# The last block of two weight tiles per unit, multiplied in float32 as it was loaded

## The chip, the cores and the metric

The kernel runs on one core of a Trainium2 chip. The metric is device time in microseconds of one execution, lower being better; times are the median of several executions, and one further execution was taken with the hardware profiler.

## The reference, cut to what matters

A two-layer trunk on 256 tokens of width 1024 ends in a mixture of eight experts, of which each token takes two. What the change touches is this sum over the experts:

```python
logits = (t @ w_router).astype(F32)
top_val, top_idx = lax.top_k(logits, TOP_K)
top_w = jax.nn.softmax(top_val, axis=-1)
combine = jnp.sum(jax.nn.one_hot(top_idx, N_EXPERTS, dtype=F32) * top_w[..., None], axis=1)
out = jnp.zeros_like(t)
for e in range(N_EXPERTS):
    gt, up = jnp.split(t @ w_gate_up[e], 2, axis=-1)
    y = (jax.nn.silu(gt) * up) @ w_down[e]
    out = out + combine[:, e:e + 1].astype(t.dtype) * y
```

Everything is float32; an expert's inner width is 3584, and its three matrices together are 44 MB.

## The kernel before

**Stream of weights.** All weights lie in HBM as one stream of tiles of 128 x 2048 float32 (1 MB). The class `Weights` loads them through the SP queue into a ring of buffers named `raw`, and splits each into two tiles of type float32r: `hi` is a copy made by ScalarE (L189), `lo` is `raw` minus `hi`, made by VectorE (L192). There are three `hi` and three `lo` buffers (`HL = 3`), so a tile is split at most three tiles before TensorE uses it. As soon as VectorE has subtracted, the load for that `raw` buffer is issued (L194), before TensorE has touched the tile; SP waits for VectorE there.

**Experts and units.** An expert's tokens are gathered into a tile `xs`. Its width 3584 is cut into seven units of 512 columns (`Unit`, loop at L1475). A unit takes six tiles: 0 and 1 for the gate, 2 and 3 for the up product, 4 and 5 for the down product. Each tile holds four blocks of 128 x 512. The down tiles of a unit come behind the gate and up tiles of the next one, so on the engines a round is: the previous unit's activation is folded or transposed, then tiles 0 to 3 of this unit, then tiles 4 and 5 of the previous one.

**Few and many.** The number of tokens of an expert is read into registers of TensorE, ScalarE and VectorE, and `choose` branches on it (L1160). With more than 64 tokens ("many", L1282 to L1286), each block is multiplied three times: token-hi by weight-hi, token-lo by weight-hi, token-hi by weight-lo. With 64 or fewer ("few", L1294 and L1298), the 128 stationary columns hold the hi parts of 64 tokens and their lo parts side by side, so two products do: by weight-hi (512 columns at once, L1294) and by weight-lo (two halves of 256, L1298). In the trace the first, third, seventh and eighth expert are few, the other four are many.

**The activation of a few unit.** It goes through all three engines while tiles 0 to 3 are multiplied: TensorE adds the two halves of the stationary columns with 16 float32 products by a matrix `fold` (L1387); ScalarE applies SiLU, VectorE multiplies (`act`, L1391); ScalarE makes the hi part (L1394) and VectorE the lo part (`ahm`, L1395), which tile 4 needs. These small steps stand in the engines' queues between the splits of the weight tiles: the order of VectorE is the splits of tiles 0 to 3, `act`, the split of tile 4, `ahm`, the split of tile 5.

**What sets the order.** No scheduler does: the program is in the order in which Python emits it (`next` calls `split`, then `products` emits the multiplications).

Of the kernel before, what the change touches and what calls it, by code (L numbers as in the profile page):

```python
# [30 lines left out]
NJ = FFE // 512  # L31
# [105 lines left out]
class Weights:  # L137


    def __init__(self, nc, wts, pool, order, queue, side=None):  # L140
        self.nc, self.wts, self.order, self.queue, self.side = nc, wts, order, queue, side
        self.pool, self.ring, self.turn = pool, [(pool, "raw", RAW)] * RAW, 0
        self.loads = self.splits = self.used = 0
        self.raw, self.ready, self.late = [], [], []
        self.limit = self.fine = len(order)

# [29 lines left out]

    def pieces(self, parts):
# [13 lines left out]
        def rest(c):  # L191
            self.nc.vector.tensor_tensor(out=lo[:, c:c + w], in0=raw[:, c:c + w], in1=hi[:, c:c + w].bitcast(F32), op=ALU.subtract)  # L192
            if c + w == TW:
                self.issue()  # L194
# [3 lines left out]
    def split(self, parts=1):  # L198
        if self.splits >= len(self.order):
            return  # L200
        for first, rest in self.pieces(parts):
            first()
            if self.side is not None and parts == 1:
                self.late.append(rest)
                self.side.after(3, self.catch_up)
            else:
                rest()

    def catch_up(self):
# [3 lines left out]
    def next(self, held=0):  # L213

        while self.splits < min(self.used - held + HL, self.limit):
# [54 lines left out]
def trunk(ctx, tc, xT_in, memT_in, wts, gcols, grows, rows, lbl, router, cst_in, tab_in, u_in, msk_in, out):  # L270
# [903 lines left out]

    class Gather:
# [6 lines left out]
        def onehot(self):  # L1182
# [6 lines left out]
            if self.both:  # L1189
                self.n = nc.values_load(counts[0:1, 0, self.e:self.e + 1], engines=[EngineType.PE, EngineType.Activation, EngineType.DVE],  # L1190
                                        min_val=0, max_val=S, skip_runtime_bounds_check_because="a count of the 256 tokens")
            self.x = main.tile([P, 2, KB, P], F32R, tag="hh" if self.e % 2 == 0 else "hl", name="xs")
# [80 lines left out]
    def products(n, o, st, w, ks, first, last, lead=None, also=()):  # L1273


        wh, wl = (t.rearrange("p (k n) -> p k n", k=4) for t in w)
# [13 lines left out]
        def few():  # L1290
            if lead:
                lead[1]()
            for m, k in enumerate(ks):
                T.matmul(o, lhsT=st[0][:, k], rhs=wh[:, k], start=first and m == 0, stop=False)  # L1294
            parts = (slice(0, 512),) if lead else (slice(0, 256), slice(256, 512))
            for k in ks:
                for c in parts:
                    T.matmul(o[:, c], lhsT=st[0][:, k], rhs=wl[:, k, c], start=False, stop=last and k == ks[-1] and c == parts[-1])  # L1298
# [249 lines left out]

    experts(W, pos, cr, g0, start)
# [59 lines left out]
```

## Time and profile before

| | us |
|---|---|
| median of 3 runs (1436.91 to 1437.73) | 1437.0 |
| the profiled execution, its own time | 1438.49 |
| its span, first to last instruction | 1436.3 |

| engine | busy, us | share of the span |
|---|---|---|
| PE (matmul) | 1373.1 | 96% |
| PEld (weight load) | 1231.9 | 86% |
| DVE (VectorE) | 1183.7 | 82% |
| ACT (ScalarE) | 1010.9 | 70% |
| POOL | 13.4 | 1% |

The experts run from about 500 us to 1424 us of the span. PE's busy time in a profile counts a matrix product until its modelled end, so neighbours overlap: the pace of a row of products is read from the starts of two rows, or from the length of a group less the time of its last product. An average over the span hides that few and many experts have different limits.

### The profile page before, as it was taken

How to read it: one execution, taken by the hardware profiler on the slowest of the kernel's cores; microseconds unless marked ns; L12 is line 12 of the kernel's file. 1: busy time of each engine (PE TensorE's matmuls, PEld its weight loads, DVE VectorE, ACT ScalarE, POOL GpSimd, SP SyncE). 2: the span in 40 equal slices, each digit the busy share in tenths (PEclk: the TensorE clock that was granted, in tenths of full speed). 3: DMA queues.
4: the chain of work that ended last, by engine and by line, in shares of the span. 5: the costliest groups of instructions: out<-in, count | busy, mean ns of one | idle time of the engine just before them, and what ended most of it. 6: DMA issues, size and time to landing. Idle time of an engine off the chain costs nothing.

```text
span 1436.3 us, 23628 instructions
## 1 busy us (share of the span) xinstructions
PE 1373.1 (96%) x8719; PEld 1231.9 (86%) x8719; DVE 1183.7 (82%) x1194; ACT 1010.9 (70%) x1104; POOL 13.4 (1%) x21
## 2 busy tenths in 40 slices
PE   8999999999999999999999999999999999999986
PEld 7989999999999888888887888888888888888875
DVE  7875655556776699998899999889899988999997
ACT  5775434435844698877787987777777778899795
POOL 0000000000000000000000000000000000000000
PEclk9999999999999999999999999999999999999999
DMA  9333455545425599999999999999999999999991
GB/s 347 145 118 144 170 189 190 190 176 206 147 89 220 206 354 390 409 388 367 354 376 405 383 416 375 345 362 350 361 367 360 369 337 376 386 403 420 405 396 38
DMA packets 64179, 431.91 MB, mean 301 GB/s; under 512 B 7504, under 2 KB 8144, under 8 KB 13584
## 3 DMA queue, kind: packets, MB, share of 16 engines
q1 hardware_dynamic: 63792, 428.63, 77.5%
q8 instruction: 109, 1.79, 0.5%
q0 software_dynamic: 224, 1.05, 0.2%
q14 instruction: 54, 0.44, 0.1%
HBM read 428.60 MB, written 1.05 MB: 299 GB/s over the span
## 4 chain that ended last, share of the span: by engine, by line
PE 50%; DVE 5%; issue 5%; DMA 3%; ACT 1%; DVEq 0%; ACTq 0%; POOL 0%; SPq 0%
PE pa L1282 7%; PE pa L1284 7%; PE pa L1286 7%; PE pb L1294 4%; DVE lo L192 4%; PE pb L1298 3%; PE pb L1282 3%; PE pa L1294 3%; PE pb L1286 3%; PE pb L1284 3%; PE pa L1298 3%; DMA raw<-in_wts 3%; PE pc L1387 3%; PE pc L1376 1%; ACT hi L189 1%
## 5 line engine op out<-in xcount | busy, mean ns | idle before, releaser
L192 DVE TENSOR_TENSOR lo<-raw,hi 128x2048 fp32r<-128x2048 f32 (+2 forms) x423 | 919.6, 2192 | 120.6 <-ACT hi L189 115.5
L189 ACT ACTIVATE hi<-raw 128x2048 fp32r<-128x2048 f32 (+2 forms) x423 | 770.7, 1838 | 172.3 <-PE pa L1284 51.6
L1298 PEld LDWEIGHTS pa<-lo,xs 128*128 128x128 f32 x800 | 113.1, 189 | 14.6 <-DVE lo L192 3.9
L1294 PE MATMUL pa<-hi,xs 128*128 128x512 f32 x448 | 124.7, 399 | 0.8 <-issue 0.6
L1298 PE MATMUL pa<-lo,xs 128*128 128x256 f32 (+1 forms) x800 | 124.7, 295 | 0.6 <-DVE lo L192 0.5
L1282 PE MATMUL pa<-hi,xs 128*128 128x512 f32 x448 | 123.8, 398 | 0.0
L1284 PE MATMUL pa<-hi,xs 128*128 128x512 f32 x448 | 120.2, 390 | 0.0
L1286 PE MATMUL pa<-lo,xs 128*128 128x512 f32 x448 | 120.1, 390 | 0.0
L309 PE MATMUL pa<-dh,lo 128*128 128x256 f32 x352 | 99.2, 282 | 1.3 <-DVE lo L192 1.3
L1284 PEld LDWEIGHTS pa<-hi,xs 128*128 128x128 f32 x448 | 84.1, 188 | 18.2
L1286 PEld LDWEIGHTS pa<-lo,xs 128*128 128x128 f32 x448 | 84.1, 188 | 18.0
L307 PE MATMUL pa<-dh,hi 128*128 128x256 f32 x352 | 99.4, 282 | 0.0
L308 PE MATMUL pa<-dl,hi 128*128 128x256 f32 x352 | 99.1, 281 | 0.0
L1282 PEld LDWEIGHTS pa<-hi,xs 128*128 128x128 f32 x448 | 81.2, 188 | 15.2
L1294 PE MATMUL pb<-hi,ahm 128*128 128x512 f32 x224 | 66.0, 416 | 28.4 <-DVE ahm L1395 27.5
L307 PE MATMUL pa<-hh,hi 128*128 128x256 f32 x288 | 84.9, 295 | 7.5 <-ACT hi L189 6.9
L1294 PEld LDWEIGHTS pa<-hi,xs 128*128 128x128 f32 x448 | 78.2, 189 | 13.4 <-issue 1.5
L308 PE MATMUL pa<-hl,hi 128*128 128x256 f32 x288 | 82.6, 287 | 0.1
L309 PE MATMUL pa<-hh,lo 128*128 128x256 f32 x288 | 82.6, 287 | 0.0
L1294 PEld LDWEIGHTS pb<-hi,ahm 128*128 128x128 f32 x224 | 39.7, 196 | 38.9 <-issue 27.2
L1298 PEld LDWEIGHTS pb<-lo,ahm 128*128 128x128 f32 x448 | 63.5, 196 | 5.8 <-DVE lo L192 0.4
L309 PEld LDWEIGHTS pa<-dh,lo 128*128 128x128 f32 x352 | 66.3, 188 | 1.5 <-DVE lo L192 1.5
(295 smaller groups left out, 2402.2 us busy)
## 6 DMA issues: line engine op xcount, KB each, us to landing
raw<-in_wts SPq DMA_DIRECT2D x393, 1024.0 KB, 7.0
raw<-in_wts SPq DMA_DIRECT2D x14, 512.0 KB, 8.0
raw<-in_wts SPq DMA_DIRECT2D x16, 256.0 KB, 6.0
xT<-in_xT SPq DMA_DIRECT2D x4, 256.0 KB, 4.9
memT<-in_memT SPq DMA_DIRECT2D x1, 1024.0 KB, 13.4
out<-res SPq DMA_DIRECT2D x4, 256.0 KB, 2.7
uc<-in_utab POOLq DMA_DIRECT2D x1, 576.0 KB, 4.5
gain<-in_grows SPq DMA_DIRECT2D x4, 128.0 KB, 7.7
```

Of the source, the lines that this page charges most:

```text
L189: self.nc.scalar.activation(hi[:, c:c + w], raw[:, c:c + w], AF.Copy)
L192: self.nc.vector.tensor_tensor(out=lo[:, c:c + w], in0=raw[:, c:c + w], in1=hi[:, c:c + w].bitcast(F32), op=ALU.subtract)
L307: T.matmul(o, lhsT=sh, rhs=mh, start=first, stop=False)
L308: T.matmul(o, lhsT=sh, rhs=ml, start=False, stop=False)
L309: T.matmul(o, lhsT=sl, rhs=mh, start=False, stop=last)
L1282: T.matmul(o, lhsT=st[0][:, k], rhs=wh[:, k], start=first and m == 0, stop=False)
L1284: T.matmul(o, lhsT=st[1][:, k], rhs=wh[:, k], start=False, stop=False)
L1286: T.matmul(o, lhsT=st[0][:, k], rhs=wl[:, k], start=False, stop=last and m == len(ks) - 1)
L1294: T.matmul(o, lhsT=st[0][:, k], rhs=wh[:, k], start=first and m == 0, stop=False)
L1298: T.matmul(o[:, c], lhsT=st[0][:, k], rhs=wl[:, k, c], start=False, stop=last and k == ks[-1] and c == parts[-1])
L1376: T.transpose(out=self.o[:, f * P:(f + 1) * P], in_=self.su[:, f * P:(f + 1) * P], identity=ident)
L1387: T.matmul(self.o[:, m * n + f * HALF:m * n + (f + 1) * HALF], lhsT=src[:, f * P:(f + 1) * P], rhs=fold, start=True, stop=True)
```

## The change

In an expert with few tokens, tiles 1 and 4 of each unit are split only in their first three blocks (1536 of 2048 columns). The last block is multiplied in plain float32 from `raw`, by the same stationary columns read as float32; that product comes first in the tile. Two of the tile's three remaining weight-hi products are cut into halves of 256 columns, which makes the number of instructions twelve as before. Since the width of the split now hangs on the expert, the split of tiles 1 and 4 stands in a branch of its own on all three engines, for every expert. And since TensorE now reads `raw`, the next load into a buffer is emitted only after the tile's products have been emitted (`refill` in `next`), for all tiles of the experts.

```diff
@@ class Weights @@
+        self.refills, self.whole = 0, None
...
+    def refill(self):
+        self.refills += 1
+        self.issue()
...
         def rest(c):
             self.nc.vector.tensor_tensor(out=lo[:, c:c + w], in0=raw[:, c:c + w], in1=hi[:, c:c + w].bitcast(F32), op=ALU.subtract)
-            if c + w == TW:
-                self.issue()
+            if c + w == TW and self.whole is None:
+                self.refill()
...
     def split(self, parts=1):
         if self.splits >= len(self.order):
+            return
+        if self.whole is not None and parts == 1 and self.whole(self.order[self.splits], self.split_most):
             return
...
+    def split_most(self, choose):
+
+        raw = self.raw[0]
+        self.pieces(1)
+        hi, lo = self.ready.pop()
+        self.ready.append((hi, lo, raw))
+
+        def parts(c):
+            self.nc.scalar.activation(hi[:, :c], raw[:, :c], AF.Copy)
+            self.nc.vector.tensor_tensor(out=lo[:, :c], in0=raw[:, :c], in1=hi[:, :c].bitcast(F32), op=ALU.subtract)
+
+        choose(lambda: parts(TW), lambda: parts(TW - 512))
...
     def next(self, held=0):
 
+
+        while self.whole is not None and self.refills < self.used:
+            self.refill()
         while self.splits < min(self.used - held + HL, self.limit):
...
@@ products @@
-        wh, wl = (t.rearrange("p (k n) -> p k n", k=4) for t in w)
+
+        wh, wl, *raw = (t.rearrange("p (k n) -> p k n", k=4) for t in w)
+        assert not raw or ks == ALL4 and lead is None
...
-            for m, k in enumerate(ks):
-                T.matmul(o, lhsT=st[0][:, k], rhs=wh[:, k], start=first and m == 0, stop=False)
-            parts = (slice(0, 512),) if lead else (slice(0, 256), slice(256, 512))
-            for k in ks:
+            halves = slice(0, 256), slice(256, 512)
+            parts = (slice(0, 512),) if lead else halves
+            if raw:
+                T.matmul(o, lhsT=st[0][:, 3].bitcast(F32), rhs=raw[0][:, 3], start=first, stop=False)
+            split = ks[:3] if raw else ks
+            for m, k in enumerate(split):
+                for c in halves if raw and m else (slice(0, 512),):
+                    T.matmul(o[:, c], lhsT=st[0][:, k], rhs=wh[:, k, c], start=first and m == 0 and not raw, stop=False)
+            for k in split:
                 for c in parts:
-                    T.matmul(o[:, c], lhsT=st[0][:, k], rhs=wl[:, k, c], start=False, stop=last and k == ks[-1] and c == parts[-1])
+                    T.matmul(o[:, c], lhsT=st[0][:, k], rhs=wl[:, k, c], start=False, stop=last and k == split[-1] and c == parts[-1])
...
@@ before the experts @@
+    def whole(t, split):
+
+        n = count_of[(t - NT) // (6 * NJ)]
+        if (t - NT) % 6 not in (1, 4) or n is None:
+            return False
+        split(lambda many, few: choose(n, many, few))
+        return True
+
+    W.whole = whole
     experts(W, pos, cr, g0, start)
```

The order on VectorE shows it between the two steps of a unit's activation. Both arms of a branch stand there, many first and few second; `act` and `ahm` are the two steps of a few unit, `pads` belongs to many. Before:

```order
L1391 TENSOR_TENSOR act<-pc,act 128x256 [waits Activation_49]
L1164 UNCONDITIONAL_BRANCH
L192 TENSOR_TENSOR lo<-raw,hi 128x2048 [waits DMAHW6_49,PE_49,Activation_49]
L1164 COMPARE_AND_BRANCH
L1173 COPY pads<-few 128x1
L1164 UNCONDITIONAL_BRANCH
L1395 TENSOR_TENSOR ahm<-act,ahm 128x4x64 [waits Activation_49]
```

And now, at the same place:

```order
L1424 TENSOR_TENSOR act<-pc,act 128x256 [waits Activation_49]
L1187 UNCONDITIONAL_BRANCH
L1187 COMPARE_AND_BRANCH
L225 TENSOR_TENSOR lo<-raw,hi 128x2048 [waits DMAHW6_49,PE_49,Activation_49]
L1187 UNCONDITIONAL_BRANCH
L225 TENSOR_TENSOR lo<-raw,hi 128x1536 [waits DMAHW6_49,PE_49,Activation_49]
L1187 UNCONDITIONAL_BRANCH
L1187 COMPARE_AND_BRANCH
L1196 COPY pads<-few 128x1
L1187 UNCONDITIONAL_BRANCH
L1428 TENSOR_TENSOR ahm<-act,ahm 128x4x64 [waits Activation_49]
```

The split of tile 4 keeps its place and its waits; it now stands in two widths inside a branch.

On TensorE, tile 1 of a unit (`pa` is the sum in PSUM, `xs` the tokens), both arms, before:

```order
L1164 COMPARE_AND_BRANCH
L1282 MATMUL pa<-hi,xs 128x512 x4
L1284 MATMUL pa<-hi,xs 128x512 x4
L1286 MATMUL pa<-lo,xs 128x512 x4
L1164 UNCONDITIONAL_BRANCH
L1294 MATMUL pa<-hi,xs 128x512 x4
L1298 MATMUL pa<-lo,xs 128x256 x8
```

And now, with the empty branch of the next whole tile's split behind it:

```order
L1187 COMPARE_AND_BRANCH
L1310 MATMUL pa<-hi,xs 128x512 x4
L1312 MATMUL pa<-hi,xs 128x512 x4
L1314 MATMUL pa<-lo,xs 128x512 x4
L1187 UNCONDITIONAL_BRANCH
L1324 MATMUL pa<-raw,xs 128x512
L1328 MATMUL pa<-hi,xs 128x512
L1328 MATMUL pa<-hi,xs 128x256 x4
L1331 MATMUL pa<-lo,xs 128x256 x6
L1187 UNCONDITIONAL_BRANCH
L1187 COMPARE_AND_BRANCH
L1187 UNCONDITIONAL_BRANCH x2
```

The arm for many is unchanged; in the arm for few one product from `raw` leads, and three products fewer use the last block's split.

On SP, the queue of the loads, six loads of the experts' stretch before:

```order
L157 DMA raw<-in_wts 128x2048 [waits DMAHW3_49,DVE_49]
L1164 UNCONDITIONAL_BRANCH
L157 DMA raw<-in_wts 128x2048 [waits DMAHW4_49,DVE_49]
L1164 UNCONDITIONAL_BRANCH
L157 DMA raw<-in_wts 128x2048 [waits DMAHW5_49,DVE_49]
L1164 UNCONDITIONAL_BRANCH
L157 DMA raw<-in_wts 128x2048 [waits DMAHW6_49,DVE_49]
```

And now:

```order
L158 DMA raw<-in_wts 128x2048 [waits DMAHW3_49,DVE_49]
L1187 UNCONDITIONAL_BRANCH x2
L158 DMA raw<-in_wts 128x2048 [waits DMAHW4_49,PE_49]
L1187 UNCONDITIONAL_BRANCH
L158 DMA raw<-in_wts 128x2048 [waits DMAHW5_49,DVE_49]
L1187 UNCONDITIONAL_BRANCH
L158 DMA raw<-in_wts 128x2048 [waits DMAHW6_49,DVE_49]
L1187 UNCONDITIONAL_BRANCH x2
```

The loads behind a whole tile wait for TensorE instead of VectorE, and the loads queued after them on SP stand behind that wait.

## Rows read from the trace of the kernel before

**Rows 1.** Windows: few, few, many, last two few; us, PE, PEld, DVE, ACT, POOL, PEclk, DMA, GB/s
```profile
500.60:602.40 101.80, 94.19 (x596) 83.80 (x596) 95.25 (x67) 90.11 (x80) 0.00 (x0) 0.98 0.95 373
724.30:833.70 109.40, 101.72 (x630) 89.99 (x629) 103.22 (x76) 93.41 (x82) 0.00 (x0) 0.98 0.99 389
833.70:1203.20 369.50, 369.50 (x1725) 307.16 (x1724) 329.57 (x230) 278.27 (x247) 0.00 (x0) 1.00 0.95 363
1203.20:1401.80 198.60, 183.21 (x1147) 162.81 (x1146) 191.17 (x138) 171.72 (x147) 0.00 (x0) 0.99 1.00 399
```

**Rows 2.** Windows of one unit each, of few experts, the same columns
```profile
724.30:740.50 16.20, 15.01 (x90) 13.18 (x89) 14.80 (x11) 13.54 (x12) 0.00 (x0) 1.00 0.98 364
740.50:755.70 15.20, 15.05 (x93) 13.20 (x92) 15.20 (x14) 13.21 (x11) 0.00 (x0) 1.00 0.97 365
755.70:770.90 15.20, 13.45 (x86) 11.82 (x85) 14.79 (x10) 12.81 (x10) 0.00 (x0) 1.00 0.99 398
770.90:787.80 16.90, 15.11 (x85) 13.00 (x84) 16.44 (x14) 13.13 (x11) 0.00 (x0) 0.90 1.01 421
787.80:805.20 17.40, 16.88 (x115) 15.29 (x114) 14.33 (x12) 15.22 (x20) 0.00 (x0) 1.00 0.97 381
...
1325.70:1344.20 18.50, 16.68 (x94) 14.54 (x93) 18.50 (x16) 14.08 (x11) 0.00 (x0) 0.91 1.02 411
...
1358.20:1372.70 14.50, 13.18 (x85) 11.85 (x84) 14.08 (x10) 12.84 (x11) 0.00 (x0) 1.00 1.02 422
```

**Rows 3.** Waits in that last unit: waiting engine and line, releaser: us, times, longest
```profile
PE pb L1294 <- DVE ahm L1395: 1.3, 1, 1.3
```

**Rows 4.** Waits over all experts, 500.6 to 1401.8 us
```profile
PE pb L1294 <- DVE ahm L1395: 26.0, 20, 1.8
...
DVE lo L192 <- DMA raw<-in_wts: 3.5, 8, 0.9
```

**Rows 5.** Timeline, plain few unit: start us, us, engine, line, instructions, [idle before]
```profile
1358.85 1.92 ACT L189 ACTIVATE hi<-raw 128x2048 fp32r<-128x2048 f32 x1 [0.55 <-PE pa L1294]
...
1359.56 1.07 PE L1294 MATMUL pa<-hi,xs 128*128 128x512 f32 x4
...
1360.46 1.11 PE L1298 MATMUL pa<-lo,xs 128*128 128x256 f32 x8
...
1361.42 1.09 PE L1294 MATMUL pa<-hi,xs 128*128 128x512 f32 x4
...
1363.55 0.42 DVE L1391 TENSOR_TENSOR act<-pc,act 128x256 f32<-128x256 f32 x1
1363.88 2.28 DVE L192 TENSOR_TENSOR lo<-raw,hi 128x2048 fp32r<-128x2048 f32 x1
...
1366.08 0.42 DVE L1395 TENSOR_TENSOR ahm<-act,ahm 128x256 fp32r<-128x256 f32 x1
...
1366.65 1.16 PE L1294 MATMUL pb<-hi,ahm 128*128 128x512 f32 x4 [1.32 <-DVE ahm L1395]
...
1371.32 1.06 PE L1387 MATMUL pc<-fold,svm 128*128 128x64 f32 x8
```

**Rows 6.** Timeline, then line view, of a float32 product of 256 columns
```profile
26.41 0.59 PE L366 MATMUL pc<-dg,cst 128*128 128x256 f32 x2
...
L366 PE MATMUL pc<-dg,cst x8: 377/378/483, 26.4 to 354.4; 128*128 128x256 f32 x8
```

**Rows 7.** Splits by tile, last two experts: ns min/median/max; the shortest have 1024 columns
```profile
L189 ACT ACTIVATE hi<-raw x82: 1049/1912/1977, 1201.1 to 1401.1; 128x2048 fp32r<-128x2048 f32 x76, 128x1024 fp32r<-128x1024 f32 x6
L192 DVE TENSOR_TENSOR lo<-raw,hi x79: 1217/2284/2294, 1203.1 to 1400.5; 128x2048 fp32r<-128x2048 f32 x76, 128x1024 fp32r<-128x1024 f32 x3
```

**Rows 8.** Loads in the plain unit
```profile
DMA packets 830, 6.09 MB, mean 419 GB/s; under 512 B 88, under 2 KB 88, under 8 KB 88
```

**Rows 9.** Branches in the stretch of three many experts, ns min/median/max
```profile
L1164 PEldq COMPARE_BRANCH  x276: 65/172/344, 848.8 to 1202.5; - x138
```

**Rows 10.** Window inside the unit at 770.9, columns of rows 1
```profile
779.00:784.00 5.00, 3.79 (x14) 3.40 (x15) 4.59 (x5) 5.00 (x4) 0.00 (x0) 0.67 1.02 423
```

More of the change, by code (lines that the diff above doesn't have):

```diff
@@ L1173, in pad_dve @@
         V.tensor_copy(pads[:, 8:9], one)
+    count_of = {}
     class Gather:
@@ L1191, in onehot @@
                                         min_val=0, max_val=S, skip_runtime_bounds_check_because="a count of the 256 tokens")
+                count_of[self.e] = self.n
             self.x = main.tile([P, 2, KB, P], F32R, tag="hh" if self.e % 2 == 0 else "hl", name="xs")
```

## The prediction

> **What bounds the kernel now.** I read the windows by stage first. Experts with many tokens are bound by TensorE: in the three that follow each other PE is busy for all of the 369.5 us [rows 1]. The change leaves the products of those units alone, so their pace should stay. The four few experts take 101.8 + 109.4 + 198.6 = 409.8 us, of which PE is busy 379.1: it stands idle for 30.7 us. That idle time is all that the change can win, beside a slow clock in it.
>
> Next, one unit at a time [rows 2]. A plain few unit (the row at 1358.2; eight others look like it, at 14.5 to 15.5 us) takes 14.5: VectorE is busy 14.1, PE 13.2, ScalarE 12.8. PE stands still once, for 1.3 us, at the first down product, which waits for `ahm` from VectorE [rows 3]; over all experts this wait has 26.0 us in 20 places [rows 4]. The timeline shows why [rows 5]: `act` comes at 1363.55 behind the split of tile 3, then the split of tile 4 runs from 1363.88 for 2.28 us, then `ahm` at 1366.08, and PE, done with tile 3, starts tile 4 at 1366.65 after 1.32 us idle. So a few unit is bound by VectorE's queue, and PE is next, only 1.3 us behind. Weights bind nothing: VectorE waited for a load 3.5 us in all [rows 4].
>
> Units with more to do differ. At 740.5 (scatter of the last expert) and 787.8 (gather of the next) PE is busy 15.05 of 15.2 and 16.88 of 17.4. At 770.9 (a one-hot to build on VectorE) and 1325.7 the granted clock averages 0.90 and 0.91 [rows 2]; inside the first of them it is 0.67 over 5 us, a mixture of the levels 2.4 and 1.2 GHz, just after PE has stood still [rows 10]. A third unit, in the first expert, is like it.
>
> **The change part by part.** *Splits.* 1536 columns lie midway between the 1024 and 2048 that have rows [rows 7]: VectorE (1217 + 2284)/2 = 1.75 us, 0.53 less; ScalarE (1049 + 1912)/2 = 1.48, 0.43 less. Per unit, with two such tiles, VectorE falls to about 13.0 us and ScalarE to 12.0.
>
> *The float32 product.* No row has one of 512 columns. The nearest is L366, 256 columns: the one instruction shows as two records, 0.59 us together, and one alone takes 0.378 [rows 6]; so the second begins 0.21 us after the first. For 512 columns I double that: two records of 0.43, 0.85 us. It replaces one weight-hi product, (1360.46 - 1359.56)/4 = 0.225, and two weight-lo halves of (1361.42 - 1360.46)/8 = 0.12 each [rows 5]; cutting two other products into halves adds 4 x 0.12 - 2 x 0.225 = 0.03. Net +0.85 - 0.225 - 0.24 + 0.03 = **+0.42 us of PE per whole tile**. Bounds: the weight load of such a product is hidden beside L366, but where float32 products are short it sets the pace, 1.06/8 = 0.13 us each (L1387 [rows 5]). Two loads wholly unhidden would make it +0.68. From below: L366's records follow each other 0.21/0.12 as slowly as float32r products of as many columns; from 0.225 that ratio gives 2 x 0.39 = 0.79, or +0.36. I take +0.42, since a product of 512 columns covers a load better than one of 256 does. There are 28 few units, 56 such tiles, less four that are split before the switch is set or belong to the last eight tiles, which are split in pieces: 52, so 22 us of PE work against 30.7 us of idle time.
>
> *The wait for ahm.* PE reaches tile 4 0.42 us later (tile 1 is longer). `ahm` comes earlier: by 0.53 from tile 4's shorter split, and by up to 0.53 more from tile 1's, if the split of tile 3 can start earlier. It can: its ScalarE half runs 1358.85 to 1360.77 [rows 5], VectorE's half ended only with `act`'s start at 1363.55, so began about 1361.3; 0.5 us are there. So 1.32 - 0.42 - 0.53 - 0.5 is below zero; the wait goes, PE is late next. A plain unit then lasts 13.2 + 0.84 = 14.05; I write 14.2, for what the chain may leave: 0.34 less, in nine units.
>
> *The clock.* In the units at 770.9 and 1325.7 and the first expert's, the longer idle stretch shrinks by the same 1.45 us. I expect the clock to stay at 2.4 GHz there: waits of 1.3 us in plain units don't lower it now (1.00 [rows 2]). Without the slow stretch PE's work at 770.9 would be a plain unit's 13.2, plus 0.84, plus about a microsecond behind the one-hot: 15.1 against 16.9, twice. At 1325.7 it has the products of the unit at 740.5: 15.05 + 0.84, with 0.3 to spare 16.2 against 18.5.
>
> *Where PE binds already* it only loses. Three gather units: 16.9 + 0.84 + 0.1 = 17.8 against 17.2 on average, +0.6 each. The two scatter units at 740.5 and its like: +0.7, but the units behind them, which waited 1.8 us (13.45 busy of 15.2), go to 14.3: -0.2 a pair. Units at a border of few and many have one whole tile and no wait to win: four times +0.4.
>
> *Branches and loads.* Each engine takes two more branches a unit. In many experts PE has seven a unit already, 276 records of 65 to 344 ns in some 21 units, 1.9 to a branch, on its sequencer [rows 9], with no idle time at all [rows 1], so they run ahead of the array; the same holds on VectorE beside splits of 2 us. Only behind the short `act` might 0 to 0.2 us show: 26 x 0.05, +1. The next load waits for TensorE's first product of a whole tile rather than VectorE's split, some 1 to 4 us later of a ring that VectorE practically never waits for: nothing, unless the lead is used up (below).
>
> A page's rule speaks against the branches. The Trainium skill, Runtime: NRT & Kernel Launch, section Instruction fetch mechanics, says that a taken branch out of the fetched window stalls the engine for a fetch; by it every added branch would cost. This trace disagrees as far as it reaches, with 369.5 us busy of 369.5; the sum stands on the rows.
>
> *The sum:* plain units 9 x -0.34 = -3.1; slow-clock units -1.8 -1.8 -2.3 = -5.9; pairs 2 x -0.2 = -0.4; gathers +1.8; borders +1.6; branches +1.0. Together -5.0, so the profiled span of 1436.3 becomes 1431.3. Its execution took 1438.49, 1.5 above the median of 1437.0; the difference carried to the median gives **1432.0 us**.
>
> **The rivals.** *The chain stays late.* If `act` hangs on something that doesn't move (ScalarE starts tile 3's copy only when PE frees a buffer, 0.55 us idle [rows 5]), VectorE's chain wins 0.53 alone: the wait becomes 1.32 - 0.42 - 0.53 = 0.37, a plain unit 14.4 (9 x -0.1), and the clock still falls (3 x -0.5); pairs turn to +0.3 each. -0.9 - 1.5 + 0.6 + 1.8 + 1.6 = +1.6: 1438.6. For it: VectorE and ScalarE wait for each other and for PE's buffers. Against it: the gap between 1360.77 and 1361.3.
>
> *The float32 product costs more* (slower). If both its weight loads show, 52 x 0.26 = 13.5 more: 1445.5. It decides from 0.1 us a tile (5.0/52). Against: the two records of L366 follow at 0.21 us, which their columns fill.
>
> *Branches show on PE* (slower): 112 branches of 1.9 records at 0.17 (the median [rows 9]) are 36: 1468 at most, were the skill's rule to hold.
>
> *Loads bind.* A unit's 6.29 MB at 419 GB/s [rows 8] take 15.0 us, longer than my 14.2. What carries the few experts is the lead that the many leave. If it runs out in the last two, their gain (3.6) goes: 1435.6. By the skill's HBM Reference (Specifications), a core's share is 358 GB/s, 17.6 us a unit, while a core alone gets about 425; this trace agrees with the second.
>
> *It doesn't do what it says* (no expert takes the branch): 1437. The few rows in four experts speak against it.
>
> *More comes back:* no idle time left in few units but at their borders, 1426.5.
>
> **How the numbers follow.** Chances: forecast 0.45 (its own range 1428.5 to 1434), more back 0.10, late chain 0.20, loads 0.05, no effect 0.03, costlier product 0.12, branches 0.05. A measurement can tell about 0.2%, 2.9 us, from no change: faster (below 1434.1) 0.55, within 0.28, slower 0.17. The range of 1426 to 1443 leaves out the branches, most of the costlier product, and little below.
>
> **What would show it.** Right: the line of `raw` products shows two records each at 0.43 us; splits of 1536 columns take 1.75 and 1.48 us; the wait of the first down product for `ahm` falls from 26 us to under 8; the granted clock is 1.00 in the one-hot units; gather units get longer; PE stays busy all through the many experts. Wrong: a wait for `ahm` that stays, waits for loads in the last expert, idle PE in many experts, or records of `raw` products further apart than 0.5 us.

## The result, and the profile after

| | before | after |
|---|---|---|
| median, us | 1437.29 | 1426.33 |
| lowest to highest of 4 runs | 1436.91 to 1437.73 | 1425.91 to 1426.99 |
| span of the profiled execution | 1436.3 | 1424.1 |

The ratio of after to before is 0.9924, with a 95% interval of 0.9907 to 0.9941: faster by 11 us. The forecast was 1432.0, in a range of 1426 to 1443; the time is at the low end of the range, below the 1428.5 to 1434 of the forecast itself, and all but equal to the rival "more comes back" (1426.5), which had a chance of 0.10.

By stage, cut where the work of [rows 1] stands (columns as there):

```profile
500.60:598.87 98.27, 96.71 (x609) 83.19 (x609) 88.87 (x67) 85.16 (x81) 0.00 (x0) 1.00 0.94 374
721.20:827.00 105.80, 104.05 (x643) 89.38 (x642) 97.00 (x76) 88.57 (x82) 0.00 (x0) 1.00 0.99 402
827.00:1196.93 369.93, 369.93 (x1726) 307.22 (x1725) 328.55 (x230) 277.60 (x247) 0.00 (x0) 1.00 0.93 363
1196.93:1389.60 192.67, 190.33 (x1172) 162.60 (x1171) 178.57 (x137) 161.79 (x147) 0.00 (x0) 1.00 1.01 409
```

The three many experts still keep PE busy throughout; the 0.4 us more there belongs to the border with the few expert ahead of them. The few experts together take 396.7 us instead of 409.8, and PE, busy for 391.1 of them, stands idle for 5.7 us where it stood for 30.7.

One unit at a time, from the start of one unit's fold to that of the next. In order: a gather, the two of a pair (scatter, then the unit behind it), a one-hot unit, the first unit of the last expert that was slow, and a plain one:

```profile
551.03:568.71 17.68, 17.42 (x118) 15.29 (x117) 15.24 (x13) 14.71 (x19) 0.00 (x0) 1.00 1.01 416
735.14:750.80 15.66, 15.66 (x95) 13.43 (x94) 14.88 (x14) 13.02 (x12) 0.00 (x0) 1.00 0.96 370
750.80:764.64 13.84, 13.84 (x88) 11.87 (x87) 12.55 (x10) 11.57 (x10) 0.00 (x0) 1.00 0.97 388
764.64:779.53 14.89, 14.07 (x89) 11.92 (x88) 13.89 (x13) 12.02 (x11) 0.00 (x0) 1.00 1.01 412
...
1314.93:1331.32 16.39, 15.91 (x97) 13.36 (x96) 16.39 (x16) 13.46 (x13) 0.00 (x0) 1.00 1.01 417
1345.39:1359.39 14.00, 14.00 (x88) 11.91 (x87) 13.05 (x10) 12.02 (x11) 0.00 (x0) 1.00 1.02 421
```

The plain unit takes 14.00 us and PE is busy for all of it; before it took 14.5, with 1.3 of idle PE [rows 2]. The clock is 1.00 in the two units that showed 0.90 and 0.91.

Waits over all experts, the lines that answer [rows 4]:

```profile
PE pb L1324 <- issue: 3.2, 5, 0.8
...
DVE lo L197 <- DMA raw<-in_wts: 2.7, 3, 0.9
...
DVE lo L225 <- DMA raw<-in_wts: 1.1, 1, 1.1
```

No line names a wait of PE for `ahm` any more; it was 26.0 us. In part only the name is lost: the first product of tile 4 is now the one from `raw` (L1324), for which the profile names no releaser ("issue"), and in half of the few units it starts 0.10 us after `ahm` is done, as in the timeline below. What PE idles ahead of it is 3.2 us in five places. VectorE's waits for loads are 3.8 us, as before (3.5). Splits and float32 products by tile (L224 and L225 hold both arms; L1324 is the product from `raw`):

```profile
L224 ACT ACTIVATE hi<-raw x108: 1470/1905/1926, 507.0 to 1379.1; 128x2048 fp32r<-128x2048 f32 x56, 128x1536 fp32r<-128x1536 f32 x52
L225 DVE TENSOR_TENSOR lo<-raw,hi x108: 1745/2278/2294, 509.2 to 1381.0; 128x2048 fp32r<-128x2048 f32 x56, 128x1536 fp32r<-128x1536 f32 x52
...
L1324 PE MATMUL pa<-raw,xs x52: 590/591/595, 511.9 to 1377.4; 128*128 128x512 f32 x52
```

There are 52 short splits, 26 of tile 1 and 26 of tile 4, of 1.47 and 1.75 us at their shortest. The line of L1324 holds tile 1's 26 products, with two records each. Last, the timeline of the plain unit, the counterpart of [rows 5]:

```profile
1349.03 1.02 PE L1324 MATMUL pa<-raw,xs 128*128 128x512 f32 x2
...
1349.48 1.27 PE L1328 MATMUL pa<-hi,xs 128*128 128x512 f32 x5
...
1350.59 0.88 PE L1331 MATMUL pa<-lo,xs 128*128 128x256 f32 x6
...
1351.31 1.09 PE L1328 MATMUL pa<-hi,xs 128*128 128x512 f32 x4
...
1352.63 0.42 DVE L1424 TENSOR_TENSOR act<-pc,act 128x256 f32<-128x256 f32 x1
1352.97 1.75 DVE L225 TENSOR_TENSOR lo<-raw,hi 128x1536 fp32r<-128x1536 f32 x1
...
1353.14 0.42 ACT L1427 ACTIVATE ahm<-act 128x256 fp32r<-128x256 f32 x1 [0.58 <-DVE act L1424]
...
1353.46 0.67 ACT L1389 ACTIVATE sgm<-pa,cs 128x512 f32<-128x512 f32 x1
...
1354.04 1.90 ACT L194 ACTIVATE hi<-raw 128x2048 fp32r<-128x2048 f32 x1
...
1354.63 0.41 DVE L1428 TENSOR_TENSOR ahm<-act,ahm 128x256 fp32r<-128x256 f32 x1
...
1355.15 1.10 PE L1324 MATMUL pb<-raw,ahm 128*128 128x512 f32 x2
...
1355.97 2.29 DVE L197 TENSOR_TENSOR lo<-raw,hi 128x2048 fp32r<-128x2048 f32 x1 [0.92 <-ACT hi L194]
...
1366.63 0.42 DVE L1424 TENSOR_TENSOR act<-pc,act 128x256 f32<-128x256 f32 x1
```

Two records of 0.59 us that take 1.02 together start 0.43 apart. The whole tile 1 lasts from 1349.03 to 1351.31, 2.28 us; before, a tile's products took from 1359.56 to 1361.42 [rows 5], 1.86: the product costs PE 0.42. And VectorE now waits 0.92 us ahead of tile 5's split, for ScalarE; before, in the unit of [rows 5], it was 0.39:

```profile
1366.89 2.29 DVE L192 TENSOR_TENSOR lo<-raw,hi 128x2048 fp32r<-128x2048 f32 x1 [0.39 <-ACT hi L189]
```

### The profile page after: what moved, and what is told of

The parts are those of the page before. It is cut to its first block, busy times and chain, and to the rows that moved or that the text cites. A ratio compares the mean times of both kernels' runs of the same rounds, so it can differ in the third digit from the quotient of the medians.

```text
span 1424.1 us, 24320 instructions
## 1 busy us (share of the span) xinstructions
PE 1386.0 (97%) x8771; PEld 1230.6 (86%) x8771; DVE 1156.5 (81%) x1194; ACT 989.8 (70%) x1104; POOL 13.4 (1%) x21
## 4 chain that ended last, share of the span: by engine, by line
PE 62%; issue 1%; DVE 1%; ACT 1%; POOL 0%; DVEq 0%; ACTq 0%
PE pa L1310 7%; PE pa L1312 7%; PE pa L1314 7%; PE pa L1328 7%; PE pa L1331 6%; PE pb L1310 4%; PE pb L1314 4%; PE pb L1312 4%; PE pc L1420 3%; PE pb L1331 3%; PE pb L1328 3%; PE pb L1324 2%; PE pa L1324 2%; PE pc L1409 1%; PE pc L1225 1%
## 5 line engine op out<-in xcount | busy, mean ns | idle before, releaser
L197 DVE TENSOR_TENSOR lo<-raw,hi 128x2048 fp32r<-128x2048 f32 (+2 forms) x315 | 677.1, 2159 | 125.2 <-ACT hi L194 120.7
L194 ACT ACTIVATE hi<-raw 128x2048 fp32r<-128x2048 f32 (+2 forms) x315 | 567.5, 1810 | 141.6 <-PE pa L1312 42.9
L225 DVE TENSOR_TENSOR lo<-raw,hi 128x2048 fp32r<-128x2048 f32 (+1 forms) x108 | 219.0, 2027 | 10.0 <-ACT hi L224 8.7
L224 ACT ACTIVATE hi<-raw 128x2048 fp32r<-128x2048 f32 (+1 forms) x108 | 184.8, 1711 | 43.9 <-PE pb L1312 19.1
L1328 PE MATMUL pa<-hi,xs 128*128 128x512 f32 (+1 forms) x474 | 129.8, 397 | 0.5 <-issue 0.3
L1310 PE MATMUL pa<-hi,xs 128*128 128x512 f32 x448 | 123.8, 398 | 0.0
L1312 PE MATMUL pa<-hi,xs 128*128 128x512 f32 x448 | 120.2, 390 | 0.0
L1331 PE MATMUL pa<-lo,xs 128*128 128x256 f32 (+1 forms) x748 | 117.7, 295 | 0.5 <-DVE lo L197 0.5
L1331 PEld LDWEIGHTS pa<-lo,xs 128*128 128x128 f32 x748 | 105.8, 189 | 10.2 <-DVE lo L197 0.9
L1328 PEld LDWEIGHTS pa<-hi,xs 128*128 128x128 f32 x474 | 79.9, 189 | 22.9 <-issue 13.6
L1314 PEld LDWEIGHTS pa<-lo,xs 128*128 128x128 f32 x448 | 84.1, 188 | 18.0
L1328 PE MATMUL pb<-hi,ahm 128*128 128x512 f32 (+1 forms) x250 | 66.5, 391 | 2.4 <-ACT hi L194 2.4
```

What stands on the lines that cost most here:

```text
L194: self.nc.scalar.activation(hi[:, c:c + w], raw[:, c:c + w], AF.Copy)
L224: self.nc.scalar.activation(hi[:, :c], raw[:, :c], AF.Copy)
L225: self.nc.vector.tensor_tensor(out=lo[:, :c], in0=raw[:, :c], in1=hi[:, :c].bitcast(F32), op=ALU.subtract)
L1312: T.matmul(o, lhsT=st[1][:, k], rhs=wh[:, k], start=False, stop=False)
L1314: T.matmul(o, lhsT=st[0][:, k], rhs=wl[:, k], start=False, stop=last and m == len(ks) - 1)
L1328: T.matmul(o[:, c], lhsT=st[0][:, k], rhs=wh[:, k, c], start=first and m == 0 and not raw, stop=False)
```

## Two theories

**TensorE.** What the prediction held: the two short splits together took the wait for `ahm` away, and TensorE's own work (0.42 us longer for each whole tile) is what a few unit takes now.

**Row A.** A few unit is paced by a closed row of steps that VectorE and ScalarE hand to each other: `act` (VectorE), hi part of `ahm`, `sgm`, hi part of tile 5 (ScalarE), then lo parts of tiles 5, 0, 1, 2, 3 (VectorE), and `act` again. In the timeline above: `act` at 1352.63, tile 5's lo part at 1355.97 (3.34 later), the next `act` at 1366.63 (10.66 later), 14.00 in all; before, 3.34 and 11.20. Tile 1's lo part is in it, tile 4's stands beside it (VectorE would only wait longer ahead of tile 5). So half of the change, tile 1's 0.53 us, would bring all of a plain unit's gain: 14.53 to 14.00, with TensorE near its bound by chance. In the experiments that ran first this theory is called "round".

The totals of the experiments also hold what lies ahead of the first few unit's fold. In the profiled executions this fold starts at 507.96 us before, at 508.15 after, and between 508.64 and 513.53 in the others; from 500 to 510 us the granted clock is 1.00 in some and 0.84 to 0.88 in others. The lengths of units don't hold that.

The lengths that the experiments gave, in us, from the first product of one unit's fold to that of the next (from the timelines; the plain unit is the last expert's fifth, the one-hot units those of the first and third expert, the border unit is the third expert's first):

| | plain | one-hot, one-hot | gather | border |
|---|---|---|---|---|
| before | 14.53 | 16.90, 16.96 | 17.16 | 15.24 |
| after | 13.98 | 14.91, 14.89 | 17.68 | 15.26 |
| branches alone | 14.54 | 16.99, 15.43 | 17.21 | 15.25 |
| float32 product, full splits | 14.59 | 15.21, 15.45 | 17.67 | 15.28 |
| short splits, no float32 product | 13.99 | 14.90, 14.90 | 17.17 | 15.25 |
| tile 4 alone | 14.55 | 15.44, 15.44 | 17.57 | 15.25 |
| tile 1 alone | 14.19 | 14.72, 14.89 | 17.18 | 15.28 |
| short split on VectorE alone | 14.06 | 14.67, 14.68 | 17.68 | 15.28 |
| before, `sgm` one step later | 14.63 | 15.53, 15.53 | 17.21 | 15.26 |
| tile 1 alone, `sgm` one step later | 14.18 | 14.81, 15.01 | 17.15 | 15.28 |
| tile 3 alone | 14.01 | 14.91, 14.89 | 16.84 | 14.38 |
| before, copies behind tiles 0 and 1 | 14.67 | 15.29, 15.27 | 17.84 | 15.38 |
| tile 3 alone, copies behind tiles 0 and 1 | 14.43 | 14.75, 14.75 | 17.62 | 14.38 |
| tile 3 alone, copies placed anew | 13.75 | 14.30, 14.41 | 16.83 | 14.39 |

## The experiments

### Parts of the change

**Branches alone.** Both arms split in full, and no product takes `raw`; the branches and the later loads stay.

```diff
-        self.ready.append((hi, lo, raw))
+        self.ready.append((hi, lo))
...
-        choose(lambda: parts(TW), lambda: parts(TW - 512))
+        choose(lambda: parts(TW), lambda: parts(TW))
```

> The splits of tiles 1 and 4 stand in their branches and the loads are issued late, as in the changed kernel, but both arms split all 2048 columns and no float32 product is made: the products are those of before. All theories that put the gain on the shorter splits: plain few units stay at 14.5 us, the wait for ahm at about 26 us in all, 1437 us within 2. If later loads or the branches themselves moved something: away from 1437 by more than 3 us, and many units off their 16.8.

Measured: 1437.34 us, ratio to before 0.9997 (0.9988 to 1.0007). The plain unit is 14.54: branches and later loads cost nothing that can be seen. The clock was the surprise. Windows of three units, the first expert's one-hot, the third's, and the slow one of the last:

```profile
538.26:555.25 16.99, 15.19 (x86) 13.06 (x85) 16.52 (x14) 13.84 (x12) 0.00 (x0) 0.90 0.99 396
769.86:785.29 15.43, 13.64 (x87) 11.72 (x85) 14.95 (x13) 12.88 (x11) 0.00 (x0) 1.00 1.01 419
1323.32:1340.26 16.94, 15.12 (x95) 13.20 (x94) 16.94 (x16) 14.35 (x13) 0.00 (x0) 1.00 1.02 418
```

The first runs at 0.90 as in the kernel before; in the other two the clock did not fall, though PE idles as long (1.8 us) and no work was taken away. 1.5 us of what each such unit can win is thus the clock's, and it does not take this change to win it. (In the last expert the unit behind it gave 1.1 us back, 14.00 to 15.12, so the total hardly moved.)

**The float32 product without the short split.** Both arms split in full; the block is multiplied from `raw` all the same.

```diff
-        choose(lambda: parts(TW), lambda: parts(TW - 512))
+        choose(lambda: parts(TW), lambda: parts(TW))
```

> The float32 product is made as in the changed kernel, but all 2048 columns are split as before. Theory shorter splits: nothing is gained, plain few units stay at 14.5 us (the added 0.4 us per tile goes into the idle time of TensorE), units bound by TensorE pay: 1440 to 1443 us. Rival, that the float32 product itself brings the gain, since it comes first in the tile, needs no split and fills TensorE's wait: near 1427.

Measured: 1440.27 us, ratio 1.0017 (1.0007 to 1.0027), as expected: the product by itself brings nothing. Where TensorE is not the bound it hides (plain 14.59, +0.05); where it is, it costs 0.3 to 0.6 (gather 17.67). The three units that had the slow clock ran at 1.00 here, at 15.21, 15.45 and 16.92 us, which hides a part of the price in the total.

**The short split without the float32 product.** The last block of a whole tile is left out of the sum; the third block is multiplied again in its place, so that the number and kind of products are those of before.

```diff
-            if raw:
-                T.matmul(o, lhsT=st[0][:, 3].bitcast(F32), rhs=raw[0][:, 3], start=first, stop=False)
-            split = ks[:3] if raw else ks
...
+            blocks = (0, 1, 2, 2) if raw else ks
```

> Splits of 1536 columns as in the changed kernel, no float32 product: the third block is multiplied a second time in the place of the last, so TensorE's work is that of before (the last block of tiles 1 and 4 is left out of the sum in few experts). Theory round: VectorE and ScalarE go round from act over the copy of tile 5 to the splits of tiles 5, 0, 1, 2, 3 and back to act, 14.53 us, of which only tile 1's split got shorter, by 0.53: plain units 14.0, and no cost on TensorE, about 1423 us. Theory TensorE: with the wait for ahm gone a plain unit lasts TensorE's 13.1 to 13.4 us: 1414 to 1417.

Measured: 1423.59 us, ratio 0.9903 (0.9887 to 0.9920). The plain unit, as a window, and its wait of TensorE:

```profile
1357.16:1371.15 13.99, 13.49 (x86) 11.77 (x85) 13.04 (x10) 12.01 (x11) 0.00 (x0) 1.00 1.01 413
```

```profile
PE pb L1324 <- DVE ahm L1424: 0.4, 1, 0.4
```

Without the 0.84 us of the float32 products PE idles 0.5 us, and the unit is no shorter: 14.0. So 14.0 is not TensorE's figure, though after the change TensorE's work fills it as well.

**Tile 4 alone, tile 1 alone.**

```diff
-        if (t - NT) % 6 not in (1, 4) or n is None:
+        if (t - NT) % 6 != 4 or n is None:
```

and the same with `!= 1`.

> Only tile 4 of a unit gets the short split and the float32 product; tile 1 is as before. Theory round: tile 4's split is not in the round, VectorE only idles longer before tile 5's split (0.39 + 0.53 us); plain units stay at 14.5, units bound by TensorE pay 0.4 each: 1436 to 1439 us. Theory TensorE: the wait for ahm falls from 1.32 to 0.79, tile 4 costs 0.40: plain units 14.25 to 14.4, 1433 to 1435 us.

Tile 4 alone: 1434.35 us, ratio 0.9974 (0.9965 to 0.9984), plain unit 14.55. PE idles less ahead of tile 4 all the same, 0.91 us instead of 1.32, and 15.4 instead of 26.0 over all experts; the product that waits starts 0.10 us after `ahm` is done, so the wait has only lost its name. Tile 5's split waits 0.9 us instead of 0.39:

```profile
1366.64:1381.19 14.55, 13.64 (x88) 11.87 (x86) 13.60 (x10) 12.46 (x11) 0.00 (x0) 1.00 0.99 392
```

```profile
1376.43 0.42 DVE L1428 TENSOR_TENSOR ahm<-act,ahm 128x256 fp32r<-128x256 f32 x1
...
1376.95 1.10 PE L1324 MATMUL pb<-raw,ahm 128*128 128x512 f32 x2 [0.91 <-issue]
```

```profile
DVE lo L197 <- ACT hi L194: 0.9, 1, 0.9
```

The total lies where the theory "TensorE" had it, the plain unit does not (14.25 to 14.4). The 3 us lie in the one-hot units (15.44, no shorter than the 15.43 of branches alone at a clock of 1.00) and in the second unit of each pair (14.40 instead of 15.12), which the first form of row A had not counted.

> As the changed kernel, but only tile 1 of a unit is whole; tile 4 is split in full, in no branch. Theory round (VectorE and ScalarE hand each other the steps of a few unit in one closed row, in which only tile 1's shorter split lies): a plain few unit still takes 14.0 us, as with both tiles, since tile 4's split stands outside the round; units where TensorE binds pay for one tile instead of two (gathers +0.2 instead of +0.4). Total 1422 to 1425, faster than the changed kernel. Theory halves (each of the two short splits brings its share): the plain unit goes half the way, 14.25, and the total lies near 1431. Theory TensorE (what was won is the wait for ahm, and the float32 product is the next bound): with half its price the plain unit falls below 14.0, to 13.6.

Tile 1 alone: 1428.78 us, ratio 0.9943 (0.9926 to 0.9959), and a plain unit of 14.19. Row A had 14.0 for it and "TensorE" 13.6; "halves" (14.25, total near 1431) comes nearest, but tile 4 alone, at 14.55, did not bring its half. The timeline of the unit has a second closed row, through TensorE (ScalarE's hi part of tile 3 waits for a buffer, TensorE for `ahm`):

```profile
1364.28 1.91 ACT L194 ACTIVATE hi<-raw 128x2048 fp32r<-128x2048 f32 x1 [1.15 <-PE pa L1328]
```

```profile
1371.72 1.16 PE L1328 MATMUL pb<-hi,ahm 128*128 128x512 f32 x4 [0.54 <-DVE ahm L1428]
```

**Row B**: TensorE's hi products of tile 0 free a buffer; hi part of tile 3 (ScalarE), its lo part, `act`, tile 4's lo part, `ahm` (VectorE); then tiles 4 and 5, the fold and tile 0 on TensorE. From 1364.28 to 1371.72 are 7.44 us, and TensorE takes 6.75 from there to the point at which the next unit's tile 3 gets its buffer: 14.19. That this sums to the period is no proof of it, so the run with tile 3 below tests it. Tile 1's split is not in row B, tile 4's is; by it tile 4's short split does work after all, once tile 1's has been made.

**The short split on VectorE alone.** ScalarE copies all 2048 columns in both arms.

```diff
-            self.nc.scalar.activation(hi[:, :c], raw[:, :c], AF.Copy)
+            self.nc.scalar.activation(hi, raw, AF.Copy)
```

> As the changed kernel, but ScalarE copies all 2048 columns of tiles 1 and 4 in few experts; only VectorE's split is short (1536). Theory round: ScalarE's copy of tile 1 runs beside VectorE's splits and has slack, so the plain unit stays at 14.0 and the total within 1.5 us of the changed kernel, 1425 to 1428. Rival: it is ScalarE's shorter copies (0.43 us each) that bring act and ahm forward; then the plain unit goes back to 14.4 to 14.5 and the total to 1433 to 1437.

Measured: 1429.78 us, ratio 0.9945 (0.9929 to 0.9962), 2 us above what row A allowed, but with a plain unit of 14.06. Its profiled execution is 3.9 us longer than that of the changed kernel, and 2.9 of it lie ahead of the first fold (511.03 against 508.15), outside the few units. VectorE's shorter split carries the gain of plain units; ScalarE's shorter copy is worth 0.06 to 0.08 there, and more in units with other work (the first expert's second unit takes 14.63 instead of 13.98).

### Tile 3 instead

If row A holds, any one of tiles 0 to 3 will do; tile 3 lies in row B too.

```diff
-        if (t - NT) % 6 not in (1, 4) or n is None:
+        if (t - NT) % 6 != 3 or n is None:
```

> As the changed kernel, but only tile 3 of a unit is whole. Two closed rows of steps are told apart that the runs so far leave as candidates. Row A: act on VectorE, hi part of ahm, the copy sgm and the hi part of tile 5 on ScalarE, then VectorE's splits of tiles 5, 0, 1, 2, 3 and act again; it measured 14.0 with tile 1's split short and would be 14.0 with tile 3's. Row B: TensorE's hi products of tile 0 free a buffer, ScalarE copies tile 3's hi part into it, VectorE makes its lo part, act, the lo part of tile 4, ahm, and TensorE goes through tiles 4, 5, the fold and tile 0; it measured 14.18 with tile 1 alone whole, since tile 1 isn't in it and tile 4 was long, and a shorter tile 3 takes 0.43 and 0.53 out of it. If both hold, the plain few unit takes 14.0 and the total is 1422 to 1426 (the float32 product costs units bound by TensorE once, not twice). If row B isn't what held tile 1 alone at 14.18, tile 3 alone stays near 14.2 and the total near 1428.

Measured: **1421.85 us, ratio 0.9888 (0.9871 to 0.9904)**, the fastest of all, below both kernels, and with half the float32 products. The plain unit:

```profile
1356.41:1370.42 14.01, 13.64 (x87) 11.92 (x86) 13.59 (x10) 12.46 (x11) 0.00 (x0) 1.00 1.01 413
```

14.0 as expected of rows A and B, with 0.4 us of idle PE. Beyond that, the few experts' first units behind a many expert fell by 0.85, where the change did nothing. There PE waited 1.2 us for ScalarE before, at two such borders:

```profile
PE pb L1282 <- ACT svm L1358: 2.4, 2, 1.2
```

With tile 3 whole PE is busy for all of that unit (14.38 of 14.38, before 14.05 of 15.24). Gathers fell below before too (16.84 against 17.16), where one float32 product was to lengthen them; why is open.

### ScalarE's part of row A

These runs move ScalarE's two small copies of a few unit, `sgm` and `svm`, to later places in its queue.

**`sgm` one step later**, behind the hi part of tile 5, in the kernel before:

```diff
...
                 if h == 0:
+                    pad_act()
+                else:
                     A.activation(self.sg, self.og, AF.Copy, scale=cs[:, 1:2])
-                else:
                     A.activation(self.sv, self.ou, AF.Copy, scale=cs[:, 0:1])
```

> The kernel before with one small copy of ScalarE in a few unit (sg to sgm, 0.67 us) moved one step later in its queue, behind the copy of tile 5's hi part; no tile is whole, nothing else differs. Theory round: the copy stands between act and the hi part of tile 5, inside the closed row, so a plain few unit falls from 14.53 to 14.1 (VectorE's own 14.1 us of work is then the bound), and the total to 1430 to 1433, with no product of TensorE changed. Rival, VectorE's queue alone binds the unit (as the forecast had it: splits and small steps one behind the other): ScalarE's order is of no effect, 14.5 and 1437. Rival TensorE: the same, 1437.

Measured: 1438.15 us, ratio 1.0008 (0.9998 to 1.0017); the plain unit got longer, 14.63. As expected by the rivals, then. ScalarE's and VectorE's rows in it:

```profile
1383.47 5.51 ACT L189 ACTIVATE hi<-raw 128x2048 fp32r<-128x2048 f32 x3
```

```profile
1385.41 8.90 DVE L192 TENSOR_TENSOR lo<-raw,hi 128x2048 fp32r<-128x2048 f32 x4 [0.59 <-ACT hi L189]
```

The wait ahead of tile 5 is gone, and one ahead of tile 0 has come: both copies still stand ahead of tile 0's hi part, which the expectation had overlooked. Row A has two legs of the same length between `act` and tile 0's lo part.

**The same with tile 1 whole:**

> Tile 1 alone whole, and ScalarE's small copy moved one step later, both together. Theory round: both shorten the same closed row, so the plain unit falls to 13.5 to 13.6, where TensorE (13.06 us of pace plus 0.40 for the one float32 product) becomes the bound; total 1417 to 1421. If the two don't add up, because something else comes late first (the loads: a unit's 6.29 MB at 420 GB/s take 15.0), the plain unit stays near 14.0 or waits for loads show in the last two experts, and the total stays at 1423 to 1425.

Measured: 1428.15 us, ratio 0.9936 (0.9919 to 0.9952); plain unit 14.18, the same as with tile 1 alone, and not the 13.5 to 13.6, or 14.0, that were expected. Row B, in which the copy does not lie, gives that length. But the copy's move had not shortened row A either: from 14.63 without a short split, less 0.53, row A would be 14.10 here, so this run is no test of it.

**Both copies behind the next unit's hi parts** (`sgm` behind that of tile 0, `svm` behind that of tile 1), in the kernel before and with tile 3 alone whole:

```diff
...
-                        prev.down(c, W.next())
+                        w = W.next()
+                        if not (last and c):
+                            u.copy(c)
...
+                        prev.down(c, w)
```

> The kernel before, no tile whole; ScalarE's two small copies of a few unit stand later in its queue: sgm behind the hi part of the next tile 0, svm behind that of tile 1 (the run with sgm moved one step only left both copies ahead of the hi part of tile 0, and that leg is as long as the other one). Rows A and B: row A loses both copies, VectorE's own 14.1 us and row B's 14.2 are what is left; the plain few unit falls from 14.53 to 14.2 with TensorE's work unchanged, the total to 1431 to 1435. Rival (TensorE or VectorE alone set the pace, ScalarE's order does nothing): 14.5 to 14.6 and 1437 to 1438.

> Tile 3 alone whole, and ScalarE's two copies moved as in the run beside it. Rows A and B: row A falls to VectorE's own work, 14.1 - 0.53 = 13.6; row B to 13.2; TensorE needs 13.06 + 0.40 = 13.46. The plain few unit takes 13.6, the total 1416 to 1420, below both the kernel before and the changed one. Rival, loads: a unit's 6.29 MB at 420 GB/s take 15.0, and with units of 13.6 the lead of the loads may be used up in the last two experts: waits of VectorE for loads of more than 5 us there, and 1420 to 1424. Rival, no row but TensorE's work sets the pace: 13.5 as well, but then the run beside it shows no change.

Measured: 1447.69 us, ratio 1.0072 (1.0056 to 1.0089), and 1435.28, ratio 0.9984 (0.9975 to 0.9994): 13 and 15 us above what was expected, with plain units of 14.67 and 14.43. The edit had added a wait. Rows of ScalarE and VectorE in the first of the two:

```profile
1393.21 0.69 ACT L1367 ACTIVATE sgm<-pa,cs 128x512 f32<-128x512 f32 x1 [0.53 <-DVE pads L1173]
```

```profile
1381.07 6.97 DVE L192 TENSOR_TENSOR lo<-raw,hi 128x2048 fp32r<-128x2048 f32 x3 [0.36 <-ACT hi L189]
```

Emitted behind the step that reads `sgm` in a many expert, the copy has to wait for VectorE's place-holder (`pads`) in a few one, which stands behind tile 5's split, and tile 1's hi part waits behind it.

**Copies placed anew**, with tile 3 alone whole: `sgm` behind the hi part of tile 5, ahead of that wait; `svm` behind that of tile 1.

```diff
                 if h == 0:
+                    pad_act()
+                else:
                     A.activation(self.sg, self.og, AF.Copy, scale=cs[:, 1:2])
...
-                        prev.down(c, W.next())
+                        w = W.next()
+                        if c == (not last):
+                            u.copy()
+                        prev.down(c, w)
```

> Beside the run with tile 3 alone whole (1421.9 us, plain unit 14.0) this one differs in ScalarE's two small copies only: sgm stands behind the hi part of tile 5 and ahead of that of the next tile 0, svm behind that of tile 1. Unlike the runs before it, which moved them to where another leg was as long (sgm one step) or where sgm had to wait for VectorE's pads (both behind tile 0), neither leg of row A keeps a copy that it need not, and svm comes after the pads anyway. Worked out from the timelines from act on: hi part of tile 5 ready at 2.8 us, VectorE there at 2.95; hi part of tile 0 ready at 5.24, VectorE at 5.33; tile 1 at 7.1, VectorE at 7.5; svm ready at 7.6, TensorE's fold needs it at 7.75. So VectorE never waits: 13.6 us a plain unit (TensorE 13.46), total 1416 to 1419. Rival: row A is no cause, only what the waits happen to name, and ScalarE's order does nothing: 14.0 and 1421 to 1424.

Measured: 1423.32 us, ratio 0.9900 (0.9883 to 0.9916): the total as with tile 3 alone, where the rival had it and not row A (1416 to 1419), but the plain unit is shorter, 13.75, which the rival (14.0) does not allow (13.6 was expected):

```profile
1357.48:1371.23 13.75, 13.63 (x87) 11.92 (x86) 13.49 (x10) 12.53 (x12) 0.00 (x0) 1.00 1.01 417
```

So ScalarE's copies are on row A, and ScalarE's order does count. By the trace the last 0.15 us to 13.6 stay with tile 4's hi part, which waits for TensorE; no run tests that. The gain went in one place, the first expert's second unit, 19.02 us instead of 14.20. There `svm` has no earlier work to stand behind. ScalarE's row, and TensorE's:

```profile
511.95 0.69 ACT L1398 ACTIVATE svm<-pa,cs 128x512 f32<-128x512 f32 x1 [2.22 <-DVE pads L1196]
```

```profile
512.70 1.97 PE L1424 MATMUL pc<-fold,svm 128*128 128x64 f32 x8 [1.80 <-ACT svm L1398]
...
514.42 2.05 PE L1328 MATMUL pa<-hi,xs 128*128 128x512 f32 x4
```

```profile
513.50:518.50 5.00, 5.00 (x16) 4.13 (x16) 2.51 (x2) 2.70 (x3) 0.00 (x0) 0.50 1.02 428
```

TensorE stands still for 1.80 us, and in the 5 us of the row above the granted clock is 0.50, the lower level of 1.2 GHz. That `svm` in its old place in that one unit would give the rest back was not tried.

## Where the prediction was right and wrong

The span fell by 12.2 us, forecast 5.0. Term by term, from the units' lengths in the two traces:

| term | forecast | measured |
|---|---|---|
| nine plain units | -3.1 | -4.55 |
| three units with the slow clock | -5.9 | -6.2 |
| two pairs | -0.4 | -1.75 |
| three gathers | +1.8 | +1.2 |
| four borders | +1.6 | +0.9 |
| branches | +1.0 | 0 |
| other few units | 0 | -1.75 |

**Right by its steps:** the price of the float32 product (0.42 us of PE; records 0.43 apart), the splits (1.75 and 1.47), the wait for `ahm` (26.0 us, now 3.2 at most), the clock of 1.00 in the slow units, the gathers that get longer, and the loads, which stay in the lead with 3.8 us of waits, at 421 GB/s in the plain unit (419 before [rows 8]). Every sign that it gave is right but that of the branches, which are nothing.

**Branches.** +1.0 should have been 0: the kernel with branches alone shows it (0.9997). In the many experts PE stays busy for 369.93 of 369.93 us beside them:

```profile
L1187 PEldq COMPARE_BRANCH  x368: 65/169/334, 828.5 to 1196.3; - x184
```

The rule of the Trainium skill (Runtime: NRT & Kernel Launch, Instruction fetch mechanics) by which each taken branch out of the fetched window would stall an engine shows in neither trace: 92 more records of compare and branch than before [rows 9], and the stretch is as full as it was.

**Mis-sized: the plain unit.** "A plain unit then lasts 13.2 + 0.84 = 14.05; I write 14.2, for what the chain may leave." It lasts 14.0, -0.53 instead of -0.34 (-0.51 on average of the nine). The 0.15 set aside for the chain was not there to lose. The mechanism behind it was half right: the prediction let both short splits pull `ahm` forward and TensorE take over. The runs show that tile 1's 0.53 is what row A loses (14.0 without any float32 product), that tile 4's leaves the unit at 14.55 by itself, and that it counts only against row B, once tile 1 is short (14.19 without it). TensorE's new work fits into 14.0 with nothing to spare, and tile 4 starts 0.10 us after `ahm`, so in this kernel the limits can't be told apart; in the experiments they can.

**Mis-sized: units left out or netted.** Six few units beside the nine were forecast at nothing and won 1.75 us together: four won 0.36 to 0.62, which fits row A, and two of the last expert lost 0.08 and 0.15. In the pairs the second unit won 1.28, not the 0.9 that "go to 14.3" allowed, since it came to 13.84; the first lost 0.41, not 0.7. Gathers lost one tile's 0.42 rather than two: only tile 4 lay where TensorE binds, as tile 1 alone (gather 17.18) and tile 4 alone (17.57) show. Of the borders the two from few to many lost 0.42 each, as forecast; the two from many to few lost nothing (0.02).

**Right, but not for the reason given: the clock.** The prediction gave the slow units' 5.9 us to the shorter idle stretch. The run with branches alone has the idle stretch as it was, and two of the three units at 1.00. The kernel before had shown as much: the one-hot unit of the seventh expert, which the prediction passed over, idles for the same 1.8 us at 1.00:

```profile
1249.70:1265.20 15.50, 13.69 (x86) 11.74 (x85) 15.03 (x13) 12.95 (x11) 0.00 (x0) 1.00 1.01 420
```

From fold to fold it took 15.43 before and 14.90 after. So of each slow unit's 2.0 us about 0.5 is row A's, and 1.5 the clock's, which comes and goes with small shifts. Since the unit behind the last expert's slow one gives 1.1 back, about 3.4 of the 12.2 us are the clock's. What decides it stays open, and that all three units ran at 1.00 may be luck.

**Loose sums.** 26 x 0.05 is 1.3, not the +1 that the sum takes for branches. The upper bound of the float32 product's price, +0.68, reads 0.13 us off a row that ends with the 0.275 of its last product; the pace is (1.06 - 0.275)/7 = 0.11, the bound +0.64. The rival whose time came, "more comes back", gives 1426.5 without its terms; its condition nearly holds, with 5.7 us of idle PE left in the few experts.

## What to carry to other kernels

Where two engines hand work to each other in a closed row, only a step that lies in the row shortens it; a step beside it, even one that the trace names in a wait, gave the plain unit nothing until the next row bound. So list the row step by step from one unit's event to the same event of the next, check that the sum is the period, and see on which step each edit lies: here one whole tile in the right place (tile 3) beat two. A wait that no longer stands in the list may only have lost its name, so compare when the engine starts with when the step it needs is done. And an edit that moves a step can bring a new wait through a buffer that the other arm of a branch uses.

## What was not expected of the hardware

The granted clock of a one-hot unit fell to 0.90 or 0.91 in three of four such units in the profiled execution of the kernel before, and in one of four with branches alone, behind the same idle 1.8 us of TensorE. And in a plain unit an engine that the profile shows busy for all of it (14.00 of 14.00) is not thereby what sets its length: 13.49 of busy time gave 13.99.
